# The weights of the last four experts taken by turns, parts of those with many tokens between parts of those with few

## The chip, the cores and the metric

The kernel runs on one core of one Trainium2 chip. The metric is the time of one execution on the device in microseconds (us). Three runs of the kernel before gave 1605.47, 1600.89 and 1598.26 us, with a median of 1600.89 us.

## What is computed

The reference is a small two-layer backbone for 256 latent tokens and 256 context tokens of width 1024. Each layer has a mixer (attention, pooling, retention) and a channel mixer. The channel mixer of the second layer is a mixture of eight experts, and it is the part that matters here:

```python
def moe_ffn(t, router, wg, wu, wd):
    tf = t.reshape(-1, shape[-1])
    logits = (tf @ router).astype(jnp.float32)
    top_v, top_i = lax.top_k(logits, TOP_K)
    top_w = jax.nn.softmax(top_v, axis=-1)
    gates = jnp.sum(jax.nn.one_hot(top_i, N_EXPERTS, dtype=jnp.float32) * top_w[..., None], axis=1)
    y = jnp.zeros_like(tf)
    for e in range(N_EXPERTS):
        y = y + gates[:, e:e + 1] * swiglu(tf, wg[e], wu[e], wd[e])
    return y.reshape(shape)
```

Every token goes to two of the eight experts. An expert is `(silu(t @ wg) * (t @ wu)) @ wd` with 1024 x 2816 weights in float32. After the experts come the residual and a layer norm, and the output.

## The kernel before, in words

All weights stream from HBM once. An expert is cut into FC = 11 **units**. Unit u has a gate and up part of 128 x 4096 floats (2 MiB, tile `rgu`) and a down part of 128 x 2048 floats (1 MiB, tile `raw`), so 3 MiB = 3.146 MB. There are two buffers of each, taken by the parity of u. `load_gu(u)` and `load_d(u)` issue the loads on the SP queue; the load for unit u + 2 is issued when unit u has given its buffer up, and SP takes the loads strictly in the order in which they are written.

The kernel counts the tokens of each expert on the chip and sorts the experts into eight **places** (`CNTI`, `POSM`, `GH`). A branch (`arms`, at the end of `build`) picks one of seven programs by these counts. Places 0 to 3 are done first; places 1, 2 and 3 are done together by `group(1, [2, 3], m, ...)`, which gives place 1 up to 256 tokens (two tiles of 128) and the two small ones m = 32 or 64 tokens, and which itself takes the weights of its three experts by turns. Places 4 to 7 follow. In the two programs in question places 4 and 7 have at most 64 tokens ("few") and 5 and 6 have up to 128 ("many").

The two kinds of unit load the engines in different ways:

- A **many** unit (M below) first splits its weights into two rounded parts: ACT copies (`ghi`, `dhi`), DVE subtracts (`glo`, `dlo`), in pieces of 128 x 1024 (`split_g`, `split_d`). PE then does three products for each tile (`mm3`): 24 matmuls of 512 columns for gate and up (`gate_up`), two transposes (`flips`), 12 matmuls of 512 columns for down (`down_to`). The buffers come free with the split, before PE has used the parts.
- A **few** unit (F below) is not split. PE multiplies the raw weights as they lie in the buffer (class `Few`: 32 matmuls of 64 x 256, one transpose, 8 of 64 x 512), so that the buffers come free only when PE has read them.

The order is written out by hand in `places(todo, side)`: for each place, for each c in range(FC), one unit: the splits, the first half of gate and up, the transposes of the unit behind, up to a few steps of side work (`aside`), the second half, the down product of the unit behind. Side work is a list of generators: `scatter` of a finished expert to its tokens, `gather` of the next expert's tokens into `XE[x]`, one-hot columns (`one_hot`), and at the end `closing` for the layer norm. With `few_ends = [(4, True), (5, False), (6, False), (7, True)]` the four last experts run one after the other: 11 F, 22 M, 11 F. For an F unit `places` does act, two steps of side work, turn and down within the same unit.

```python
                if few:
                    load_gu(u + 2)
                    if u < NU - 1:
                        act(u)
                        aside(2 if c < 9 else 8)
                        turn(u)
                        aside(1)
```

The tokens of place 4 and 7 come from a stash that `gather` filled before (`from_stash`).

## Time and profile before

| what | value |
|---|---|
| median of three runs | 1600.89 us |
| the profiled execution | 1599.23 us |
| its span, first to last instruction | 1597.4 us |
| mean granted clock of TensorE | 0.983 |
| PE busy | 1478.6 us (93%) |
| DVE busy | 743.9 us (47%) |
| ACT busy | 614.9 us (38%) |
| HBM read | 395.53 MB, 248 GB/s over the span |

The profiled execution lies 1.83 us above its span and 1.66 us below the median of the three runs. The shares are means over stages that differ: DMA stands at 40 to 50% in the first half of the span and near 90 to 100% from 860 us on, where the experts run. What the change is worth has to be read from the stretch of places 4 to 7, from 1177 us to the end. A busy PE is not a PE at its peak, because matmuls are pipelined and their ends are modelled, so periods between like instructions say more than busy time.

### The profile page before, as it was taken

What the parts mean: (1) busy time and instruction counts of PE and PEld (TensorE: products, weight loads), DVE (VectorE), ACT (ScalarE), POOL (GpSimd) and SP (SyncE); (2) the same over time, 40 slices, a digit from 0 to 9 for tenths busy, and PEclk for the clock granted to TensorE, in tenths of its full rate; (3) what the DMA queues carried; (4) which work ended last, traced back from release to release, by engine and by line L of the source; (5) the groups of instructions that cost most, each with busy time, mean ns of one, the idle gap of its engine ahead of it and who ended that gap; (6) DMA issues with size and microseconds to landing.
All of it is one profiled execution on the core that took longest, in us unless ns stands there. A gap on an engine that the chain in (4) does not pass through costs nothing. (4 is left out here: it accounts for less than half of the span.)

```text
span 1597.4 us, 25278 instructions
## 1 busy us (share of the span) xinstructions
PE 1478.6 (93%) x10388; PEld 1085.5 (68%) x10388; DVE 743.9 (47%) x1435; ACT 614.9 (38%) x1122; POOL 93.8 (6%) x105
## 2 busy tenths in 40 slices
PE   6989998999999999978988799999998889999986
PEld 4646777677777788775675577777765468877643
DVE  4564456332222353576555534344233078888412
ACT  3465444522222343255552223323220066767301
POOL 2310002000000240010000100000000000000120
PEclk9999999999999999999998899999999999999998
DMA  9445333554445332151368799999999998988894
GB/s 381 176 142 202 106 106 106 200 208 171 158 170 191 114 132 99 41 180 58 154 271 366 306 378 377 353 375 371 364 368 342 378 378 308 352 337 321 342 400 192
DMA packets 45699, 398.36 MB, mean 249 GB/s; under 512 B 5601, under 2 KB 5857, under 8 KB 8961
## 3 DMA queue, kind: packets, MB, share of 16 engines
q1 hardware_dynamic: 44640, 391.98, 64.5%
q0 software_dynamic: 640, 4.26, 0.7%
q8 instruction: 85, 1.39, 0.3%
q10 hardware_dynamic: 288, 0.36, 0.1%
q14 instruction: 46, 0.37, 0.1%
HBM read 395.53 MB, written 1.05 MB: 248 GB/s over the span
## 5 line engine op out<-in xcount | busy, mean ns | idle before, releaser
L281 PE MATMUL b<-HH,wh 128*128 128x512 f32 (+1 forms) x752 | 267.6, 356 | 7.8 <-ACT wh L281 6.4
L281 PE MATMUL b<-HH,wl 128*128 128x512 f32 (+1 forms) x752 | 258.7, 344 | 0.7 <-DVE wl L281 0.6
L281 PE MATMUL b<-HL,wh 128*128 128x512 f32 (+1 forms) x752 | 258.2, 343 | 1.1 <-DVE HL L281 1.1
L281 DVE TENSOR_TENSOR wl<-raw,wh 128x512 fp32r<-128x512 f32 x228 | 150.6, 702 | 124.6 <-ACT wh L281 124.4
L281 PE MATMUL bk<-ghi,HL 128*128 128x512 f32 x528 | 182.4, 408 | 8.4 <-ACT ghi L281 8.4
L281 PEld LDWEIGHTS b<-HH,wh 128*128 128x128 f32 x752 | 143.1, 190 | 64.7 <-issue 26.4
L281 ACT ACTIVATE wh<-raw 128x512 fp32r<-128x512 f32 x228 | 132.4, 622 | 117.7 <-DMA raw<-in_fgu_dram 56.9
L281 DVE TENSOR_TENSOR glo<-rgu,ghi 128x1024 fp32r<-128x1024 f32 x132 | 154.8, 1219 | 16.0 <-ACT ghi L281 15.9
L281 PEld LDWEIGHTS b<-HH,wl 128*128 128x128 f32 x752 | 143.2, 190 | 19.0 <-DVE wl L281 2.2
L281 PEld LDWEIGHTS b<-HL,wh 128*128 128x128 f32 x752 | 143.3, 191 | 17.2 <-DVE HL L281 1.9
L281 ACT ACTIVATE hx<-bk 128x256 f32<-128x256 f32 (+3 forms) x89 | 28.3, 318 | 304.6 <-PE bk L281 304.6
L281 ACT ACTIVATE ghi<-rgu 128x1024 fp32r<-128x1024 f32 x132 | 131.2, 1051 | 18.7 <-DMA rgu<-in_moe_dram 12.9
L281 DVE TENSOR_TENSOR hx<-hx,bk 128x256 f32<-128x256 f32 (+2 forms) x88 | 29.6, 336 | 232.2 <-ACT hx L281 232.2
L281 PEld LDWEIGHTS bk<-ghi,HL 128*128 128x128 f32 x528 | 101.7, 193 | 37.2 <-ACT ghi L281 9.5
L281 PE MATMUL bk<-dhi,SP 128*128 128x512 f32 x352 | 120.1, 402 | 0.0
L281 PE MATMUL b<-h,wh 128*128 128x512 f32 (+1 forms) x384 | 112.0, 376 | 0.0
L281 PE MATMUL bk<-glo,HL 128*128 128x512 f32 x264 | 105.5, 400 | 0.8 <-DVE glo L281 0.8
L281 DVE TENSOR_TENSOR H<-H,b 128x512 f32<-128x512 f32 x22 | 15.1, 688 | 168.4 <-PE b L281 158.3
L281 DVE TENSOR_TENSOR dlo<-raw,dhi 128x1024 fp32r<-128x1024 f32 (+1 forms) x55 | 78.8, 1434 | 15.8 <-ACT dhi L281 15.8
L281 PE MATMUL bk<-rgu,hx 128*32 128x128 f32 (+1 forms) x1376 | 77.1, 305 | 4.6 <-DVE hx L281 2.9
L281 PEld LDWEIGHTS b<-h,wh 128*128 128x128 f32 x384 | 69.9, 188 | 16.3 <-issue 2.5
L281 PEld LDWEIGHTS bk<-dhi,SP 128*128 128x128 f32 x352 | 66.1, 188 | 17.3 <-issue 1.6
(335 smaller groups left out, 2169.8 us busy)
## 6 DMA issues: line engine op xcount, KB each, us to landing
rgu<-in_moe_dram SPq DMA_DIRECT2D x81, 2048.0 KB, 9.7
raw<-in_moe_dram SPq DMA_DIRECT2D x80, 1024.0 KB, 7.4
raw<-in_wmod_dram SPq DMA_DIRECT2D x40, 1024.0 KB, 4.9
raw<-in_fgu_dram SPq DMA_DIRECT2D x22, 1024.0 KB, 6.0
p<-in_moe_dram SPq DMA_DIRECT2D x16, 1024.0 KB, 14.8
raw<-in_wout_dram SPq DMA_DIRECT2D x12, 1024.0 KB, 5.0
raw<-in_fd_dram SPq DMA_DIRECT2D x11, 1024.0 KB, 4.9
raw<-in_wib_dram SPq DMA_DIRECT2D x9, 1024.0 KB, 4.9
```

Of the source, the lines that this page charges most:

```text
L281: r = f(*args, **kw)
```

## The change

The two programs with `few_ends` no longer call `places`. A new function `by_turns` runs places 4 to 7. It first makes a list of the 44 units: 37 turns in which 22 M units (place 5, then 6) stand with 15 F units (place 4, then the first four of 7) spread evenly between them, then the last seven F units of place 7 alone:

```
M5.0 M5.1 F4.0 M5.2 F4.1 M5.3 M5.4 F4.2 M5.5 F4.3 M5.6 M5.7 F4.4 M5.8 F4.5 M5.9 M5.10 F4.6 M6.0
F4.7 M6.1 M6.2 F4.8 M6.3 F4.9 M6.4 M6.5 F4.10 M6.6 F7.0 M6.7 M6.8 F7.1 M6.9 F7.2 M6.10 F7.3
F7.4 F7.5 F7.6 F7.7 F7.8 F7.9 F7.10
```

Of the 37 turns 15 end with an F: eight pairs M F and seven triples M M F. The loop body is the one order for both kinds, with act, turn and down of a unit always one unit behind, also for F. If the unit after an F is an M, the first half of that M's split is issued during the F (`early`). The tokens of a few expert are gathered on the spot (`tokens_few`, 32 matmuls of 64 columns) and not from a stash. The accumulators of 4 and 7 move to banks 3 and 2; 5 and 6 share banks 0 and 1. `group` now hands over with place 5 as its next (128 slots for one expert where two copies of 64 slots stood).

```diff
-    def split_d(u, parts=1, eng=None):
+    def split_d(u, parts=1, eng=None, w=None):
...
+        def outer(u):
+            s, c = stream[u]
+            if light(u):
+                few_of(u).down(RD[u % 2], c)
+                load_d(u + 2)
+            else:
+                down_to(B[s], part[u] % 2, hts.pop(u), c)
+            if c == FC - 1 and s != 7:
+                side.append(scatter(s))
+                next(side[-1])
+                if s == 5:
+                    side.append(places_few(7))
...
+        side += [places_few(4), places_many(6)]
+        behind = None
+        early = set()
+        for u in range(u0, NU):
+            s, c = stream[u]
+            last = u == NU - 1
+            if light(u):
+                if c == 0:
+                    tokens_few(s)
+            elif u not in early:
+                run(split_g(u, 0, 2))
+            if behind:
+                act(behind)
+            inner(u, range(0, 4))
+            if not light(u):
+                run(split_g(u, 1, 2))
+                load_gu(u + 2)
+                rows = split_d(u, 2, w=part[u] % 2)
+                next(rows)
+            if behind:
+                turn(behind)
+            if light(u) and not last and not light(u + 1):
+                early.add(u + 1)
+                run(split_g(u + 1, 0, 2))
...
+            aside(4 if u == u0 else 3 if s == 7 and c > 3 else 2)
+            inner(u, range(4, 6))
+            if behind:
+                outer(behind)
+            inner(u, range(6, 8))
+            if light(u):
+                load_gu(u + 2)
+            else:
+                run(rows)
+            behind = u
...
-    def group(s, few, m, then):
+    def group(s, few, m, then, nxt=None, x=None):
...
-                  1: lambda: places(few_ends, group(1, [2, 3], 32, True)),
-                  2: lambda: places(few_ends, group(1, [2, 3], 64, True)),
+                  1: lambda: by_turns(lambda: group(1, [2, 3], 32, False, 5, 0)),
+                  2: lambda: by_turns(lambda: group(1, [2, 3], 64, False, 5, 0)),
```

How the order moves, first on PE at the start of an F unit. Before, in place 4 (`rgu` and `raw` are the raw weights, `os` the one-hot columns of a scatter, `CA` the identity of a transpose):

```order
L281 MATMUL bk_6521<-rgu_5029,hx 64x256 x8
L281 MATMUL bk_6521<-rgu_5029,sil 64x256 x8
L281 MATMUL bk_6522<-os_6505,SP 128x256 x4
L281 MATMUL bk_6520<-os_6506,SP 128x256 x4
L281 MATMUL bk_6521<-CA,hx 128x128
L281 MATMUL bk_6522<-os_6506,SP 128x256 x4
L281 MATMUL bk_6515<-raw_79,hx 64x512 x4
```

Now, in an F of the turns, with the last products of the M ahead of it and the down product of that M (`dhi`, `dlo`) within it (three of its 12 matmuls are shown, the others read alike):

```order
L281 MATMUL bk_6519<-ghi_8973,HL 128x512
L281 MATMUL bk_6521<-rgu_5029,hx 64x256 x8
L281 MATMUL bk_6519<-CA,hx 128x128 x2
L281 MATMUL bk_6520<-og,HH 128x128 x8
L281 MATMUL bk_6521<-rgu_5029,sil 64x256 x4
L281 MATMUL bk_6515<-dhi_8977,SP 128x512
L281 MATMUL bk_6515<-dlo_8979,SP 128x512
L281 MATMUL bk_6516<-dhi_8977,SP 128x512
L281 MATMUL bk_6521<-rgu_5029,sil 64x256 x4
L281 MATMUL bk_6519<-ghi_8971,HL 128x512
```

The gate and up product of an F stood in one piece; now the transposes, a step of side work and the 12 down matmuls of the M ahead stand between its pieces.

Second, the SP queue, with what each load waits for (the row between two loads, which only forms an address, is left out). Before, in the M stage:

```order
L281 DMA rgu1_6304<-in_moe_dram 128x4096 [waits DMAHW5_49,DVE_49]
L281 DMA raw0_78<-in_moe_dram 128x2048 [waits DMAHW6_49,DVE_49]
L281 DMA rgu0_5029<-in_moe_dram 128x4096 [waits DMAHW7_49,DVE_49]
L281 DMA raw1_79<-in_moe_dram 128x2048 [waits DMAHW0_49,DVE_49]
L281 DMA rgu1_6304<-in_moe_dram 128x4096 [waits DMAHW1_49,DVE_49]
```

Now, over pairs M F:

```order
L281 DMA rgu1_6304<-in_moe_dram 128x4096 [waits DMAHW1_49,PE_49]
L281 DMA rgu0_5029<-in_moe_dram 128x4096 [waits DMAHW3_49,DVE_49]
L281 DMA raw0_78<-in_moe_dram 128x2048 [waits DMAHW2_49,PE_49]
L281 DMA raw1_79<-in_moe_dram 128x2048 [waits DMAHW4_49,DVE_49]
L281 DMA rgu1_6304<-in_moe_dram 128x4096 [waits DMAHW5_49,PE_49]
L281 DMA rgu0_5029<-in_moe_dram 128x4096 [waits DMAHW6_49,DVE_49]
```

Every second load waits for PE instead of DVE, and the down part of an F stands behind the gate and up part of the M after it.

Third, DVE at an F between two M, now (`glo` and `dlo` are splits, `hx` the activation, `SP` the split of the turned activation, `XT` the rows that a scatter adds to):

```order
L281 TENSOR_TENSOR hx<-hx,bk_6519 128x256 [waits Activation_49]
L281 TENSOR_TENSOR SP<-bk_6519,SP 128x256 [waits Activation_49]
L281 TENSOR_TENSOR glo_8976<-rgu_6304,ghi_8973 128x1024 [waits DMAHW4_49,Activation_49]
L281 TENSOR_TENSOR glo_8976<-rgu_6304,ghi_8973 128x1024 [waits Activation_49]
L281 TENSOR_TENSOR XT<-XT,bk_6520 128x2x256 [waits PE_49]
L281 TENSOR_TENSOR XT<-XT,bk_6522 128x2x256 [waits PE_49]
L281 TENSOR_TENSOR hx<-hx,bk_6521 128x128 [waits Activation_49]
```

The first half of the next M's split, which waits for that M's load, now stands ahead of the additions of a scatter and of the F's own activation.

## Rows read from the trace of the kernel before

**Rows 1.** Stages: the group, F of 4, M, F of 7, tail.
```profile
core 0: us, PE busy (x) PEld busy (x) DVE busy (x) ACT busy (x) POOL busy (x), PEclk, DMA share, GB/s
924.00:1177.00 253.00, 252.31 (x2520) 189.27 (x2516) 96.93 (x146) 79.78 (x120) 0.00 (x0) 1.00 0.93 366
1177.00:1281.00 104.00, 91.35 (x702) 54.07 (x690) 21.32 (x60) 10.63 (x27) 0.00 (x0) 0.98 0.95 369
1281.00:1481.00 200.00, 190.60 (x873) 153.21 (x870) 166.81 (x187) 139.28 (x176) 0.00 (x0) 0.98 0.89 339
1481.00:1561.00 80.00, 71.51 (x473) 42.38 (x473) 20.12 (x37) 14.57 (x27) 13.06 (x16) 1.00 0.95 373
1561.00:1597.00 36.00, 23.12 (x165) 13.38 (x161) 9.22 (x25) 5.90 (x15) 0.00 (x0) 0.88 0.42 170
```

**Rows 2.** SP queue in time: issue of `rgu` for units 44, 55, 77, 87.
```profile
1177.47 0.33 SPq L281 DMA_DIRECT2D rgu<-in_moe_dram  x1
...
1281.36 0.33 SPq L281 DMA_DIRECT2D rgu<-in_moe_dram  x1
...
1480.84 0.33 SPq L281 DMA_DIRECT2D rgu<-in_moe_dram  x1
...
1561.40 2.06 SPq L281 DMA_DIRECT2D rgu<-in_moe_dram  x2
```

**Rows 3.** Waits of the SP queue, 1290 to 1490 us (total, times, longest).
```profile
SPq L281 <- DVE glo L281: 98.4, 22, 5.9
SPq L281 <- DVE dlo L281: 81.9, 21, 5.6
```

**Rows 4.** The page: few experts' products in the group (32 slots).
```profile
L281 PE MATMUL bk<-rgu,hx 128*32 128x128 f32 (+1 forms) x1376 | 77.1, 305 | 4.6 <-DVE hx L281 2.9
```

**Rows 5.** SP queue in time: `rgu` loads in the group, three units apart.
```profile
939.83 0.82 SPq L281 DMA_DIRECT2D rgu<-in_moe_dram  x1
...
964.43 0.96 SPq L281 DMA_DIRECT2D rgu<-in_moe_dram  x1
...
989.09 0.33 SPq L281 DMA_DIRECT2D rgu<-in_moe_dram  x1
```

**Rows 6.** PE in time, one M unit (start us, us, engine).
```profile
1369.64 0.38 PE L281 MATMUL bk<-CA,hx 128*128 128x128 f32 x2
...
1372.63 0.40 PE L281 MATMUL bk<-dhi,SP 128*128 128x512 f32 x1
...
1375.44 0.39 PE L281 MATMUL bk<-ghi,HL 128*128 128x512 f32 x1
...
1378.20 0.38 PE L281 MATMUL bk<-CA,hx 128*128 128x128 f32 x2
```

**Rows 7.** PE in time, F units that run free.
```profile
1260.75 0.33 PE L281 MATMUL bk<-CA,hx 128*128 128x128 f32 x1 [0.70 <-DVE hx L281]
1261.46 1.94 PE L281 MATMUL bk<-raw,hx 128*64 128x512 f32 x8 [0.38 <-DVE hx L281]
1263.23 1.90 PE L281 MATMUL bk<-rgu,hx 128*64 128x256 f32 x16
1264.95 1.90 PE L281 MATMUL bk<-rgu,sil 128*64 128x256 f32 x16
1267.55 0.33 PE L281 MATMUL bk<-CA,hx 128*128 128x128 f32 x1 [0.70 <-DVE hx L281]
```

**Rows 8.** PE in time: two scatter steps in one row.
```profile
1200.79 1.21 PE L281 MATMUL bk<-os,SP 128*128 128x256 f32 x8
```

**Rows 9.** DVE in time: two pieces of a split.
```profile
1372.56 2.35 DVE L281 TENSOR_TENSOR glo<-rgu,ghi 128x1024 fp32r<-128x1024 f32 x2
```

**Rows 10.** SP queue in time: `rgu` loads five units apart in place 7.
```profile
1517.80 0.33 SPq L281 DMA_DIRECT2D rgu<-in_moe_dram  x1
...
1554.02 0.33 SPq L281 DMA_DIRECT2D rgu<-in_moe_dram  x1
```

**Rows 11.** Stage view, 20 us within place 7.
```profile
1540.00:1560.00 20.00, 17.52 (x129) 8.83 (x131) 1.45 (x5) 3.31 (x7) 0.00 (x0) 1.00 1.00 425
```

More of the change, by code (lines that the diff above doesn't have):

```diff
@@ L1524, in split_g @@
                 load_gu(u + 2)
-    def split_d(u, parts=1, eng=None):
+    def split_d(u, parts=1, eng=None, w=None):
         if u < NU:
+            w = u % 2 if w is None else w
             n = 2048 // parts
@@ L1530, in split_d @@
                 c = slice(n * j, n * j + n)
-                split(RD[u % 2][:, c], DHI[u % 2][:, c], DLO[u % 2][:, c], eng)
+                split(RD[u % 2][:, c], DHI[w][:, c], DLO[w][:, c], eng)
                 yield ("rest",)
@@ L2246, in group @@
             units += [(1 + i // FC, i % FC) for i in range(len(few) * c, len(few) * c + len(few))]
-        stream.update({u0 + i: (([s] + few)[j], c) for i, (j, c) in enumerate(units)})
-        end = u0 + len(units)
+        own = {u0 + i: (([s] + few)[j], c) for i, (j, c) in enumerate(units)}
+        stream.update(own)
         part.update({u0 + n * c: u0 + c for c in range(FC)})
-        nxt = s + 1 + len(few)
-        x = nxt % 2
+        if nxt is None:
+            nxt = s + 1 + len(few)
+            x = nxt % 2
         side = []
@@ L2388, in group @@
                 run(split_d(u + n))
-        stream.clear()
-        part.clear()
+        for u in own:
+            del stream[u]
+            part.pop(u, None)
         if len(few) == 1:
@@ L2540, in next_first @@
         run(split_d(FC))
-    few_ends = [(s, s in (4, 7)) for s in (4, 5, 6, 7)]
     def two_groups():
```

89 lines of the change are left out of this document (added).

## The prediction, made before the changed kernel was run

> **What bounds the kernel now.** I read the stage view first [rows 1], because the change touches only places 4 to 7, then the SP queue for when each load is issued [rows 2], then what SP waits for [rows 3], then PE's rows for the price of one unit [rows 6, 7]. The program that runs is the one with 32 slots, as the 128*32 form of the group's few products shows [rows 4], and it is one of the two that call the new function, so that the change does take effect.
>
> From the load of unit 44 to that of unit 87, the last, 383.9 us pass (1177.47 to 1561.40), 43 steps of 8.93 us [rows 2]. They fall apart into three pieces: 11 F units of place 4 in 103.9 us (9.44 each), 22 M units in 199.5 us (9.07 each), ten F units of place 7 in 80.6 us (8.06 each). Behind the last load 36.0 us are left to the end of the span.
>
> In the M piece PE is the bound: it is busy 190.6 of 200 us while DMA stands at 0.89 and moves 339 GB/s [rows 1]. There SP waits 98.4 us for the gate and up splits and 81.9 us for the down splits, at nearly every load [rows 3]. The splits in turn wait for buffers that PE still reads. One M unit takes PE 8.56 us, from one pair of transposes to the next [rows 6]; 22 of these are 188.3 us of the 199.5.
>
> In the F pieces it is the other way round. PE needs less: the down product 1.77 us, the two halves of gate and up 1.72 and 1.90, the transpose 0.33, so 5.7 us [rows 7], and idles between for activation and copy on other engines. DMA stands at 0.95 [rows 1], and at best moves 425 GB/s [rows 11]. So one stage leaves DMA waiting for PE, the other PE waiting for DMA, and the change lays them over each other.
>
> **The change part by part.** *Prices in the turns.* For DMA I take the group, which already mixes both kinds of work with the same buffers: six units in 49.26 us, 8.21 each or 383 GB/s [rows 5]. For PE: M 8.56, F 5.7, and the side work, about 45 steps in all (scatters of six results, gathers, one-hot columns) at 0.6 us by the scatter's row [rows 8], 27 us in all or 0.7 for each of the 37 turns.
>
> *A pair M F* then asks PE for 8.56 + 5.7 + 1.4 = 15.7 us and DMA for 16.4. *A triple M M F* asks PE for 22.8 + 2.1 = 24.9 and DMA for 24.6. The two are nearly equal, so neither hides fully behind the other, and I add 0.3 us to a triple for the handover. Eight pairs at 16.4 and seven triples at 25.2 are 307.6 us.
>
> *Does the buffer of an F come free in time?* It is the new wait: SP's next load for that buffer now stands behind PE. From the start of the F, PE does 1.8 us of gate and up, two transposes, some 1.2 us of side work, 0.9 of gate and up, the 12 down matmuls of the M ahead (2.81, from 1372.63 to 1375.44 [rows 6]) and 0.9 again, 7.9 us with the transposes. Behind the F's gate and up part three loads lie ahead in the queue: the next M's gate and up, the F's down part and that M's down part, 2 + 1 + 1 MiB of 3 MiB a unit, so 4/3 x 8.21 = 10.9 us. That leaves 3 us, enough for an issue but not for a stall. Queued behind the waiting load on SP are the next M's gate and up part and both down parts.
>
> *The early split.* ACT and DVE now stand at the next M's load while the F runs. Behind them wait a scatter's additions and the F's own activation, which is needed only a unit later. A gather that follows its one-hot columns in the same step would make PE wait for the split as well. There are three such places. Each costs from 0 to 4.6 us: the M's load lands when PE is half through the F, and four pieces of split and the columns must pass, two of them 2.35 us [rows 9].
>
> *Gathering on the spot* for places 4 and 7: twice 32 matmuls of 64 columns and two copies. By columns (2048, as in the eight matmuls of rows 8) 1.2 us each, by matmuls (0.15 each) 4.8. For both kinds of one-off together I take 8 us out of 2.4 to 23.4, since PE has some slack in a pair.
>
> *The last seven F alone.* Free of scatters, place 7 shows five steps in 36.22 us, 7.24 each [rows 10]. The new loop keeps one unit behind, so that PE no longer waits for activation and copy inside a unit (0.70 and 0.38 us [rows 7]); six steps of 7.24 are 43.4 us.
>
> *Edges.* The hand-over from the group gathers 128 slots for one expert instead of twice 64, the same matmuls. The first M must be split before PE can start, but its load was issued as early as before; 0, with -2 to +3 us. The tail has the same instructions, 36.0 us; the additions on POOL (13.06 us [rows 1]) have two units of 7 us before they are read. The bookkeeping in `group` costs nothing, it is done when the program is built.
>
> **Sum.** 307.6 + 8 + 43.4 = 359.0 us in place of 383.9: 24.9 us less. The profiled execution took 1599.23 us, so 1574.3; the median of the runs is 1.66 above it, and I predict **1576 us**. From here on all times are against that median.
>
> A rule speaks against this. The Trainium skill, page "DMA: Bandwidth & Descriptors", section Specifications, puts the share of HBM for one core at about 358 GB/s. By it a unit costs 8.79 us at best, the 43 steps 378 us, and with the one-offs nothing is won. The trace does not agree with it as a limit: rows 11 show 425 GB/s, rows 5 383.
>
> **Rivals.** *A: memory is already the limit.* The 43 steps carry 43 x 3.146 MB in 383.9 us, 352 GB/s. If that is what memory gives while the vector engines work, then no order helps: 0 gained, 1601 us. For it: place 4 shows 369 GB/s at a DMA share of 0.95 [rows 1], so the engines were busy and yet slow. Against it: rows 5, 10 and 11, and SP's waits for splits in the M stage [rows 3]. The rule above would put the time here as well.
>
> *B: slower, by the early split.* If in each F the steps of side work made PE wait for the split of the next M, the F's buffer would come free 4.6 us later than the 3 us in hand allow, and DMA would stand still. Fifteen times 4.6 is 69 us; against the 24.9 gained, 44 us more: 1645 us. It turns to a loss from six of the 15 F units on. For it: the order on DVE, where a scatter's additions stand behind the split. Against it: side work uses two banks in turn and two steps at a time, so PE mostly writes without waiting for the addition just queued.
>
> *C: more than forecast.* If loads run at rows 11's rate whenever issued, PE is the only bound: 22 x 8.56 + 15 x 5.7 + 27 = 300.8, with 43.4 for the rest 344.2, 39.7 less: 1561 us. Against it: PE and the loads would have to fit without a gap.
>
> **How the numbers follow.** The forecast has 0.73, C 0.09, A 0.11, B 0.07. A measurement of this kernel can tell about 0.5% (8 us) from no change. Forecast and C are faster: 0.82. A is the same: 0.11. B is slower: 0.07. The forecast's own range is 1568 to 1594: 1576 with the one-offs at 2.4 or 23.4 us and the edges at -2 or +3. C at 1561 and a margin of 3 us set the low end, 1558. The high end is 1596, which leaves A and B out, 0.18.
>
> **What would show it.** Right: the load of unit 87 some 25 us earlier after that of unit 44; in the turns a mean of about 8.5 us a unit, DMA above 0.93 and near 370 GB/s, PE above 0.93; 7.0 to 7.4 us for a unit at the end; a tail of 36 us. Wrong: DMA at 0.95 or more with 355 GB/s and PE idle (A); SP's gate and up loads waiting for PE with DMA under 0.9, and PE waiting for DVE in the F units (B).

## The result, and the profile after

The changed kernel takes 1678.61 us (median of four runs, 1677.53 to 1680.32), the kernel before 1603.18 us in its four runs. The ratio is 1.0469, with a 95% interval from 1.0442 to 1.0496: **slower by 4.7%**, where 1576 us had been forecast. The profiled execution took 1677.53 us, its span 1675.7.

First a slip in the rows ahead of the prediction. The load at 1281.36 in [rows 2] is that of unit 56; unit 55 was issued at 1273.97. So place 4 took 96.5 us (8.77 a unit) and the M stage 206.9 us (9.40 a unit), and PE's 188.3 us stand against 206.9. The sum of 383.9 us stands.

The stages of the kernel after by the stage view, for [rows 1]: the group, the hand-over, the turns, six F alone, and the last stretch.

```profile
924.00:1177.00 253.00, 252.31 (x2513) 189.12 (x2513) 97.09 (x147) 79.76 (x120) 0.00 (x0) 1.00 0.93 368
1180.00:1215.00 35.00, 30.32 (x223) 22.27 (x215) 18.54 (x27) 15.49 (x23) 0.00 (x0) 0.95 0.83 318
1215.00:1600.00 385.00, 336.29 (x1621) 219.56 (x1621) 189.05 (x250) 143.12 (x192) 1.76 (x3) 0.92 0.72 290
1600.00:1640.00 40.00, 32.79 (x214) 16.41 (x212) 3.00 (x9) 3.87 (x9) 11.31 (x14) 0.87 0.85 332
1640.00:1676.00 36.00, 22.02 (x151) 12.23 (x147) 9.23 (x25) 5.91 (x15) 0.00 (x0) 0.86 0.40 149
```

The group is what it was. In the turns PE is busy for only 336 of 385 us, DMA has fallen to a share of 0.72 and 290 GB/s, and the granted clock to 0.92. Neither side is the bound; each waits for the other. From the load of unit 44 (1180.43) to that of unit 87 (1640.56) 460.1 us pass, against 383.9 before and 359.0 forecast.

What SP waits for from 1200 to 1600 us (total, times, longest), for [rows 3]:

```profile
SPq L281 <- PE bk L281: 229.5, 29, 20.7
SPq L281 <- DVE glo L281: 85.4, 22, 6.6
SPq L281 <- DVE dlo L281: 29.5, 7, 5.9
```

The loads now wait mostly for PE, 229.5 us in all. In the M stage before they waited for splits alone [rows 3], but in the F stages they waited for PE too: in the kernel before from 1177 to 1281 and from 1481 to 1561 us, and, for comparison, in e12 (below), whose turns come close to the forecast, from 1190 to 1540 us:

```profile
SPq L281 <- PE bk L281: 92.8, 24, 7.0
SPq L281 <- PE bk L281: 57.6, 16, 6.6
SPq L281 <- PE bk L281: 198.1, 40, 10.5
```

So a long wait of SP for PE is not the loss in itself. What counts is whether DMA runs dry meanwhile, and whether what is issued then comes in time. How it fails is seen in one pair and the triple behind it, which carry no side work. The SP queue in time:

```profile
1345.04 0.33 SPq L281 DMA_DIRECT2D rgu<-in_moe_dram  x1
1351.05 0.33 SPq L281 DMA_DIRECT2D raw<-in_moe_dram  x1
1362.15 3.98 SPq L281 DMA_DIRECT2D rgu<-in_moe_dram  x2
1369.14 0.91 SPq L281 DMA_DIRECT2D raw<-in_moe_dram  x2
1378.02 3.98 SPq L281 DMA_DIRECT2D rgu<-in_moe_dram  x2
1385.02 0.91 SPq L281 DMA_DIRECT2D raw<-in_moe_dram  x2
1391.93 0.33 SPq L281 DMA_DIRECT2D rgu<-in_moe_dram  x1
1396.99 0.33 SPq L281 DMA_DIRECT2D raw<-in_moe_dram  x1
1408.72 0.33 SPq L281 DMA_DIRECT2D rgu<-in_moe_dram  x1
```

and the stage view around the holes (us, then PE, PEld, DVE, ACT, POOL, granted clock, DMA share, GB/s):

```profile
1356.00:1361.00 5.00, 5.00 (x30) 3.06 (x26) 2.79 (x3) 2.28 (x3) 0.00 (x0) 1.00 0.02 10
1370.60:1401.30 30.70, 26.43 (x118) 17.17 (x117) 15.88 (x18) 13.41 (x17) 0.00 (x0) 0.94 0.98 407
1401.30:1409.00 7.70, 7.70 (x49) 4.75 (x49) 4.48 (x6) 4.31 (x8) 0.00 (x0) 1.00 0.07 29
```

The F start at 1354.8, 1370.64 and 1401.35 us. From 1351 to 1362 and from 1397 to 1409 SP stands at one gate and up load whose buffer the F is to be multiplied from, and issues nothing. What was issued before has landed by then, and DMA does next to nothing (0.02, 0.07). In the triple that begins with the F at 1370.64 it is the other way: the loads run at 407 GB/s and still come late. The second M's gate and up part takes the F's buffer and goes out at 1378.02, when the F's last product is done, together with another load; its down part takes the F's down buffer, which is multiplied only one unit later, and goes out at 1385.02. The PE rows of this triple:

```profile
1370.64 1.95 PE L281 MATMUL bk<-rgu,hx 128*64 128x256 f32 x16
1391.57 0.62 PE L281 MATMUL bk<-ghi,HL 128*128 128x512 f32 x2
1394.56 0.50 PE L281 MATMUL bk<-dhi,SP 128*128 128x512 f32 x1 [1.92 <-ACT SP L281]
1395.88 0.84 PE L281 MATMUL bk<-dhi,SP 128*128 128x512 f32 x2 [0.59 <-DVE SP L281]
1396.95 1.06 PE L281 MATMUL bk<-dhi,SP 128*128 128x512 f32 x2
1401.35 1.95 PE L281 MATMUL bk<-rgu,hx 128*64 128x256 f32 x16
```

and ACT's:

```profile
1385.85 2.00 ACT L281 ACTIVATE ghi<-rgu 128x1024 fp32r<-128x1024 f32 x2 [3.54 <-DMA rgu<-in_moe_dram]
1393.18 1.06 ACT L281 ACTIVATE dhi<-raw 128x1024 fp32r<-128x1024 f32 x1 [3.16 <-DMA raw<-in_moe_dram]
1394.14 0.37 ACT L281 ACTIVATE SP<-bk 128x256 fp32r<-128x256 f32 x1
```

The gate and up part is there 7.8 us after its issue, the down part 8.2 us after its own. ACT stands at the late down part with the turned activation (`SP`) queued behind it, and PE stands for ACT. After this wait two products of 512 columns take 1.06 us (1396.95) where two took 0.62 before it (1391.57). From F to F the triple takes 30.7 us; forecast were 25.2.

An F with side work in it gives its gate and up buffer up much later still. In nine of the 15 F of the turns the next load goes out 7.4 us after the F's start. In the second, third and fourth F of place 4 it is 14.8, 15.7 and 15.0 us, because PE stands within the F for an addition, one-hot columns or a copy that wait on DVE behind two pieces of the early split:

```profile
1254.58 1.29 PE L281 MATMUL bk<-os,og 32*128 32x256 f32 x4 [3.81 <-DVE XT L281]
1297.22 1.95 PE L281 MATMUL bk<-og,HH 128*128 128x128 f32 x8 [4.01 <-DVE og L281]
1323.77 0.59 PE L281 MATMUL bk<-GH,og 128*128 128x2 f32 x2 [4.23 <-DVE os L281]
```

Some of the F alone at the end wait for their loads, and this one starts at half rate (1.90 us for sixteen products in [rows 7]):

```profile
1604.64 3.58 PE L281 MATMUL bk<-rgu,hx 128*64 128x256 f32 x16 [2.27 <-DMA rgu<-in_moe_dram]
```

### The profile page after: what moved, and what is told of

Same layout as the page of the kernel before. It is cut to its first block, busy times and chain, and to the rows that moved or that the text cites. A ratio compares the mean times of both kernels' runs of the same rounds, so it can differ in the third digit from the quotient of the medians.

```text
span 1675.7 us, 25208 instructions
## 1 busy us (share of the span) xinstructions
PE 1527.3 (91%) x10388; PEld 1094.9 (65%) x10388; DVE 746.0 (45%) x1437; ACT 613.6 (37%) x1116; POOL 93.9 (6%) x105
## 4 chain that ended last, share of the span: by engine, by line
PE 35%; DMA 6%; DVE 6%; ACT 2%; issue 1%; SPq 0%; DVEq 0%; ACTq 0%
PE bk L281 35%; DMA raw<-in_moe_dram 4%; DVE glo L281 2%; DMA rgu<-in_moe_dram 2%; DVE dlo L281 1%; ACT ghi L281 1%; DVE XT L281 1%; ACT dhi L281 0%; DVE rgu L281 0%; DVE hx L281 0%; ACT hx L281 0%; DVE SP L281 0%; DVE os L281 0%; DVE kept L281 0%; ACT SP L281 0%
## 5 line engine op out<-in xcount | busy, mean ns | idle before, releaser
L281 PE MATMUL bk<-ghi,HL 128*128 128x512 f32 x528 | 188.0, 415 | 10.6 <-ACT ghi L281 10.6
L281 PEld LDWEIGHTS b<-HL,wh 128*128 128x128 f32 x752 | 144.3, 192 | 17.2 <-DVE HL L281 1.9
L281 PE MATMUL bk<-dhi,SP 128*128 128x512 f32 x352 | 130.2, 432 | 13.3 <-ACT SP L281 11.3
L281 PEld LDWEIGHTS bk<-dhi,SP 128*128 128x128 f32 x352 | 70.7, 202 | 42.1 <-ACT SP L281 13.5
L281 PE MATMUL bk<-rgu,hx 128*32 128x128 f32 (+1 forms) x1376 | 84.4, 317 | 8.4 <-DMA rgu<-in_moe_dram 6.8
L281 DVE TENSOR_TENSOR H<-H,b 128x512 f32<-128x512 f32 x22 | 15.1, 688 | 169.6 <-PE b L281 158.6
L281 PEld LDWEIGHTS b<-h,wh 128*128 128x128 f32 x384 | 69.8, 188 | 16.4 <-issue 2.5
```

What stands on the lines that cost most here:

```text
L281: r = f(*args, **kw)
```

## The experiments

All times below from one run stand beside one run of the kernel before on the same chip (1597.74 to 1607.67 us), so the periods in the traces say more than differences of a few us: up to the load of unit 44 all these kernels do the same, and yet it goes out anywhere from 1176.4 to 1183.9 us. "43 steps" is the time from the load of unit 44 to that of unit 87. Kernels with e1's edit ask for that last load earlier within its unit (some 42 us are left behind it in place of 35), so the 43 steps show them some 7 us too good. "To the end" is the time from the load of unit 44 to the end of the span; it is free of both: 495.3 us in the change, 419.9 in the kernel before, 395.0 by the forecast (359.0 and 36.0).

### First round: one suspect at a time

**e1, the F's product in one piece, its next load right behind.**

```diff
-            inner(u, range(0, 4))
+            inner(u, range(0, KT if light(u) else 4))
...
+            else:
+                load_gu(u + 2)
```

> The changed kernel took 1678.6 us; in it the 37 turns take 402 us and the last six steps 58 us (issue of the gate and up load of unit 44 to that of unit 87). Theory H (held buffer): a unit with few tokens gives its gate and up buffer up only at its very end, behind the down product of the unit ahead (2.8 us) and the side work, so that loads are issued late and in a burst and PE starves. Here its gate and up product stands in one piece and its load right behind it. H expects the triples M M F to fall by about 3 us each and the last units from 9.7 to about 7.4 us: some 35 us less, about 1643 us. Theory Q (vector queue): PE starves because the early split of the next unit stands on DVE and ACT ahead of the side work. Q expects a gain only at the end, some 12 us: about 1666 us.

Measured: 1646.82 us, 32 less; to the end 468.4, 26.8 less. The total is near theory H, but not by the way H gave: clean triples (those without side work) stay at 30 to 30.4 us. The F's down buffer still comes free a unit late, and the second M's down part with it. In such a triple of e1 ACT and PE stand as in the change:

```profile
1376.19 1.06 ACT L281 ACTIVATE dhi<-raw 128x1024 fp32r<-128x1024 f32 x1 [4.42 <-DMA raw<-in_moe_dram]
1377.58 0.50 PE L281 MATMUL bk<-dhi,SP 128*128 128x512 f32 x1 [3.21 <-ACT SP L281]
```

So the late gate and up load is about a quarter of the miss, and half of what the last F lost (from the load of unit 81 to the end 93.1 us in the change, 85.9 here, 79.4 forecast), but not what the clean triples lose.

**e2, no side work in an F ahead of an M, three steps instead of two elsewhere.**

```diff
-            aside(4 if u == u0 else 3 if s == 7 and c > 3 else 2)
+            aside(4 if u == u0 else 3 if s == 7 and c > 3 else 0 if light(u) and not last and not light(u + 1) else 3)
```

> Side work is taken out of the units with few tokens that come before one with many, where the early split stands ahead of it on DVE, and is done in the others (3 steps instead of 2). Q expects the waits of PE for og, XT, os and HL on DVE (25 us in the turns) to go, and part of the lost clock with them: about 1645 us. H expects the buffer of a few unit to come free some 1.2 us earlier where a step stood ahead of it, in all at most 10 us: about 1668 us.

Measured: 1658.31 us, 20 less, between the two; to the end 15.1 less. In the three F that gave their buffer up after 14.8 to 15.7 us it is 7.4 now.

**e3, fifteen pairs and then seven M in a row.**

```diff
-            units.append((many_ if -(-2 * FC * (i + 1) // turns) > -(-2 * FC * i // turns) else few_).pop(0))
+            units.append((many_ if i % 2 == 0 or i >= 2 * (turns - 2 * FC) else few_).pop(0))
```

> The 37 turns stand as 15 pairs M F and then 7 M, in place of 8 pairs and 7 triples. In the changed kernel a pair without side work takes 15.9 to 17.1 us, a triple 29.7 to 31.0. H says that a triple loses since the load of its second M is issued only when the F ahead ends, one unit before it is needed: 7 triples less 5.3 us each, about 1641 us. Q, for which the number of F units counts, expects 1678 within 8 us.

Measured: 1657.75 us, 21 less, between the two (17.6 to the end): the triples are dear, but not the whole miss.

**e4, no early split.**

```diff
-            if light(u) and not last and not light(u + 1):
+            if False:
```

> The early split is left out: the first half of a many unit's split is issued in that unit itself, as for the other ones. Q expects the waits of PE for DVE in the few units to go: 20 to 40 us less, about 1650 us. H expects each of the 15 many units behind a few unit to start with a wait for its first pieces of split (2.3 us) and its own buffer to come free as much later: up to 35 us more, about 1710 us.

Measured: 1667.43 us, 11 less (13.5 to the end). The early split costs something; the price that was set for going without it didn't come.

### Second round: do they add up?

**e5, e1 to e3 together.**

> The three edits of the first runs together: gate and up of a few unit in one piece with its load behind it, no side work behind an early split, 15 pairs and then 7 many units. Alone they took 31.8, 20.3 and 20.9 us off 1678.6. If they remove different waits they add up to 1606 us. If two of them (one piece, pairs) remove the same one, the late load of the second many unit, some 1625 us.

Measured: 1631.36 us, 47 less where the three alone gave 73. Of these 26 us of overlap 11 lie ahead of the load of unit 44, where the edits do nothing. To the end it is 47.0 less, where the three alone gave 59.5: an overlap of some 12 us, so that they remove the same waits in part.

**e6, an F ahead of an M ends within itself**: its activation, transpose and down product come at once, and its down part is asked for ahead of the next M's loads.

```diff
+            if light(u) and not last and not light(u + 1):
+                inner(u, range(0, 4))
+                if behind:
+                    turn(behind)
+                inner(u, range(4, 8))
+                load_gu(u + 2)
+                act(u)
+                if behind:
+                    outer(behind)
+                turn(u)
+                aside(1)
+                early.add(u + 1)
+                run(split_g(u + 1, 0, 2))
+                outer(u)
+                behind = None
+                continue
```

> A few unit that comes before a many unit ends within itself: its activation, turn and down product, the load of its next down part, and one step of side work are all written ahead of the early split of the next unit; the order of units is that of the change. H and Q together expect the gain of the first run (to 1647 us) and, since down parts are loaded earlier and nothing but the next unit stands behind the early split, most of PE's remaining waits there (ACT SP 14, DVE og 12, XT 5, os 5 us): about 1615 us. If it stays at 1640 or more, neither the late down parts nor the order on the vector engines is what is left.

The F alone at the end keep e1's edit.

Measured: 1614.92 us, 64 less than the change, by the order alone. The 43 steps take 393.2 us; to the end it is 435.0, 60.2 less. Clean pairs take 15.2 us, clean triples 24.8 and 25.0. One clean triple of e6 in the stage view, beside the one above that took 30.7 us:

```profile
1338.30:1363.30 25.00, 23.94 (x120) 16.35 (x119) 15.80 (x18) 13.30 (x17) 0.00 (x0) 1.00 1.00 393
```

DMA is at 1.00 throughout. The load for the F's buffer goes out 4.2 us after the F's start (in the change 7.4), the one for its down buffer 9.7 after (in the change 14.4):

```profile
1342.53 0.33 SPq L281 DMA_DIRECT2D rgu<-in_moe_dram  x1
1347.96 0.33 SPq L281 DMA_DIRECT2D raw<-in_moe_dram  x1
```

What is left above the forecast are the turns with side work: pairs of 17.2 to 17.5 us, the pair with the tokens of place 7 23.6, triples of 29.1 to 34.1.

**e7, e6 with the pairs of e3.** Part of one scatter works on other data here; the work is the same.

> The same with 15 pairs and then 7 many units. If the triples still lose by a late load, another 15 to 20 us less than the run before, about 1598 us; if the loads are now early enough, the same as the run before within 5 us.

Measured: 1615.34 us, the same as e6. Once the F ends within itself, triples are no worse than pairs.

**e8, the changed kernel with 24 of the 32 products left out of the two gathers of tokens.**

```diff
-            for k in range(KT):
+            for k in (0, 7):
```

> The changed kernel with 24 of the 32 matmuls left out that gather the tokens of a few expert on the spot, for places 4 and 7 (so their tokens are not gathered and these two experts work on stale data). In the trace they took 3.65 and 6.51 us. Taken away, some 8 us less if they are on the path, up to 15 if the lower clock behind them goes too: 1664 to 1671 us. Not on the path: 1678 us.

Measured: 1662.64 us, 16 less; to the end 12.5 less. This gather stands on the path. Its rows in the change, at place 4 with the F behind it and at place 7, and last the F behind the shortened gather of place 4 in e8:

```profile
1221.51 3.65 PE L281 MATMUL bk<-HL,HH 128*128 128x64 f32 x32
1225.63 3.63 PE L281 MATMUL bk<-rgu,hx 128*64 128x256 f32 x16 [0.47 <-ACT hx L281]
1515.12 6.51 PE L281 MATMUL bk<-HL,HH 128*128 128x64 f32 x32 [1.57 <-DVE HL L281]
1220.61 1.95 PE L281 MATMUL bk<-rgu,hx 128*64 128x256 f32 x16 [0.47 <-ACT hx L281]
```

### Third round: the price of side work

**e9, the changed kernel without side work in the turns.**

```diff
-        side = begin()
+        begin()
+        side = []
...
-        side += [places_few(4), places_many(6)]
```

> The changed kernel with the side work of the turns left out: the steps that the group hands over, the one-hot columns and gathers of places 4 to 7, and the scatters of places 4, 5 and 6. Only the on-the-spot gathers of tokens, the last scatter and the closing stay, so the output is not the reference's. The order of units, splits, products and loads is as changed. Theory S (side work is not hidden: each step stands where the F's buffer is waited for, or ahead of it on DVE, and so costs more than its time on PE): pairs of the kind that run clean in the changed kernel, 16.0 us, everywhere, and triples of 30.2, so eight times 16.0 and seven times 30.2 = 339 us with the two gathers of tokens some 350 in place of 402 for the turns; the time about 50 us less, 1625 to 1632. Theory H (side work costs its time on PE, 45 times 0.6 = 27 us, as the forecast had it): 1650 to 1654. If it were hidden: 1675 or more.

Measured: 1626.11 us, 52 less, and the 43 steps take 412.2 (to the end 447.2, 48.0 less). Theory S. Pairs are 15.8 to 16.1 us everywhere (one, with the tokens of place 7, 20.0), triples 29.5 to 32.6.

**e10, e6 with the tokens gathered ahead as side work.**

```diff
-            og, b = ogs[s], BK[7]
+            og, b = ogs[s], B[s][0]
...
+                if k % 2:
+                    yield
```

> The kernel whose F ahead of an M ends within itself (1614.9 us, e6), with the tokens of places 4 and 7 gathered ahead, step by step as side work, into the idle accumulator bank of that expert; only the two copies stay at the first F. Theory O (the gather on the spot costs because PE waits for its one-hot columns and its copies in one place, with no load going out): 12 to 16 us less than e6 for the two, 1599 to 1603. Theory P (it is PE time, wherever it stands): 1610 to 1615.

Measured: 1620.75 us; to the end 441.4, where e6 has 435.0. Not theory O, and above the range of theory P: the pair with the tokens of place 7 falls from 23.6 to 16.6 us, but the turns that now hold its steps grow by as much or more (29.4 to 34.0, 15.2 to 17.4).

**e11, three F of place 4 ahead of the turns.** A bank that the group's last scatter still reads is written early here; the work is the same.

> As e10 for place 7, but three F of place 4 stand ahead of the turns, so that 34 turns are left (22 M, 12 F) and the side work that the group hands over falls where F stand alone and PE has time to spare. If side work is what keeps e6 above its forecast, and not the mixing: 1595 to 1605. If an F alone costs what the last seven do (7.2 us with the loads as bound) and side work costs the same anywhere: 1608 to 1616. The kernel before on the same chip is what it stands against.

Measured: 1612.38 us, in the second of the two ranges: side work costs about the same there. The 43 steps, 392.0 us, are those of e6.

**e12, e6 without side work**: the edits of e6 and e9.

> The kernel whose F ahead of an M ends within itself (e6, 1614.9 us), with the same side work left out as in e9, so that the output is not the reference's. Theory S (what keeps e6 above its forecast is side work alone, and the two causes add up): every pair 15.2 and every triple 25.0 as in e6's clean turns, 297 us with the tokens some 305 in place of 352 for the turns, and the time 1565 to 1575. Theory M (pairs and triples are dearer for another reason while the group's rest drains, such as DMA or the banks that 5 and 6 share): the first turns stay at 17 and 31 to 34 us, and the time is 1590 or more.

Measured: 1586.32 us, 11 above the upper end of theory S and below theory M. The pairs are as expected, 15.2 and 15.3 us, the triples 24.8 to 26.9, the one pair with tokens 19.3; the 37 turns, by their loads, take 318.7 us where some 305 had been expected (and 315.6 forecast). The 43 steps take **359.6 us; the forecast was 359.0**. That flatters it: to the end it is 401.5 us against 395.0, since 41.9 us follow the last load in place of 36.0. Besides, the load of unit 44 goes out at 1183.11 us, 5.6 later than before. The stage view over the turns, first of e9, from its first F to the last of the turns:

```profile
1218.20:1536.60 318.40, 283.91 (x1366) 179.84 (x1366) 163.53 (x192) 134.29 (x175) 0.00 (x0) 0.97 0.81 327
```

and the same stretch of e12, with the same instructions:

```profile
1225.00:1504.90 279.90, 267.90 (x1368) 178.67 (x1368) 161.63 (x192) 134.01 (x175) 0.00 (x0) 0.99 0.94 372
```

With the F ended within itself DMA stands at 0.94 and PE at 268 of 280 us: both near full, as forecast. And 12 us of idle PE are too little room for 27 us of side work (the forecast's estimate).

Why a step costs more than its products is seen in e6's rows. PE by line, the sided triple from 1240.7 to 1274.7 us (busy, mean ns of one | idle before and what ended it):

```profile
L281 PE MATMUL bk<-ghi,HL 128*128 128x512 f32 x33 | 13.2, 463 | 0.0
L281 PE MATMUL bk<-os,og 32*128 32x256 f32 x16 | 2.4, 333 | 1.8 <-DVE XT L281 1.7
L281 PE MATMUL bk<-IDR,og 128*128 128x128 f32 x2 | 0.4, 302 | 1.9 <-DVE XT L281 1.9
L281 PE MATMUL bk<-GH,og 128*128 128x2 f32 x2 | 0.4, 260 | 0.5 <-DVE os L281 0.5
```

and the clean one from 1338.3 to 1363.3:

```profile
L281 PE MATMUL bk<-ghi,HL 128*128 128x512 f32 x33 | 11.0, 397 | 0.0
```

DVE in time, in the sided triple:

```profile
1249.09 4.62 DVE L281 TENSOR_TENSOR glo<-rgu,ghi 128x1024 fp32r<-128x1024 f32 x4
1253.63 1.22 DVE L281 TENSOR_TENSOR dlo<-raw,dhi 128x1024 fp32r<-128x1024 f32 x1
1254.77 0.74 DVE L281 TENSOR_TENSOR XT<-XT,bk 128x256 f32<-128x256 f32 x2
```

and the stage view of the 6 us behind the first wait:

```profile
1256.00:1262.00 6.00, 6.00 (x21) 4.70 (x22) 4.58 (x6) 2.36 (x5) 0.00 (x0) 0.72 0.94 332
```

Of the 9 us between the two triples PE is busy for 5.8 (29.71 against 23.94 us) and idle for 3.2 (4.2 us of waits against 1.0). The busy part is 3.2 us of side products and some 3.6 us by which the same weight products take longer (the `ghi` alone 2.2); the groups overlap a little, so that they add up to more than 5.8. PE waits because a scatter's addition to `XT`, which gives the bank back, stands behind five pieces of split on DVE (1249.09 to 1254.77). After the wait the granted clock is 0.72 over 6 us.

**e13, the steps of an M issued one by one, later in the unit.**

```diff
-            aside(4 if u == u0 else 3 if s == 7 and c > 3 else 2)
+            aside(4 if u == u0 else 3 if s == 7 and c > 3 else 2 if light(u) else 0)
...
+            if heavy_side:
+                aside(1)
```

The last two lines stand twice, ahead of the down product of the unit behind and after the last quarter (`heavy_side`: an M that isn't the first unit).

> e6 with the same side work, but the two steps of an M are issued one by one, between the last quarters of its gate and up product and behind them, in place of both in a row right behind its splits. Theory D (a step is dear because its addition stands behind the splits on DVE, so that PE waits 1.7 to 1.9 us for a bank at the next step and then runs at the lower clock): the waits of PE for XT and og go, sided triples fall from 29 to 34 us to 27 to 29, and the time to 1598 to 1606. Theory W (side work costs its matmuls and DVE time wherever it stands): 1612 to 1617.

Measured: 1611.34 us, just below theory W's range; the 43 steps 388.0 us, 5.2 less than e6. PE's waits for `XT` and `og` are gone from the turns, as D said, but the gain is well below what D gave: in their place stand 8.4 us of waits for splits (`glo`, 3.7 in e6), and sided triples still take 28 to 32 us.

### Last round: what is left of the order by turns

**e14 and e15, e13 with the tokens of place 7 gathered ahead.** In both the gather for place 4 is left out: it was tied to the first unit, and the first F is the third unit. e15's expectation, written before this was seen, blames a bank.

```diff
+                    if u == u0:
+                        run(tokens_few(s))
+                    tokens_copy(s)
```

> e13 (1611.3 us, and 13.6 above the kernel before on the same chip) with the tokens of place 7 gathered ahead as side work into the idle accumulator bank, as in e10. The pair that holds this gather falls from 22.2 to about 17 us, so 4 to 6 us less than e13. Theory L (loads and PE are both near their limit in the turns, and side work, hidden by the slack of PE in the F stages of the kernel before, has to be paid for there): it stays 5 to 12 us above the kernel before. If the order by turns still held a gain that only stalls take away: below the kernel before.

> As e14, but the tokens of place 4 go to the bank that the change uses for them, since the group's last scatter still reads the other one, which e14 overwrites. The same work in the same order: 1600 to 1606 us, ratio to the kernel before 0.996 to 1.004 (theory L: the gain of the order and the price of the side work cancel). A ratio below 0.995 would speak for a gain that is left in the order by turns.

Measured: e14 1602.98 us, ratio 0.9998 [0.9978, 1.0017]; e15 1602.17 us, 0.9995 [0.9980, 1.0010]. Level with the kernel before, with some work missing.

**e16, e15 with three F of place 4 first** (here the first F is the first unit, and its tokens are gathered).

> e15 with three F of place 4 ahead of the turns, as in e11, so that part of the side work stands where PE has slack. If that is what the side work lacks in the turns: 4 to 10 us less than e15, 0.993 to 0.998 of the kernel before. If an F alone with side work costs as much as it saves: the same as e15 within 3 us.

Measured: 1614.34 us, ratio 1.0068 [1.0044, 1.0091]. Part of what it has above e15 is the gather, but e17 below, with the same work, is lower still. Taking F out of the turns for side work gains nothing.

**e17, e15 with the gather for place 4 back.** The edit against e15:

```diff
-                    if u == u0:
+                    if s == 4:
```

> e15 does not gather the tokens of place 4 at all (32 matmuls, two copies, in the first F); here they are gathered as in the changed kernel, so that no work is left out. By the 16 us for most of two such gathers in the changed kernel (e8), and the 5 for one in a mended pair (e13's 22.2 against e14's 16.9), 5 to 8 us more than e15: 1607 to 1611, ratio to the kernel before 1.003 to 1.006. Theory L (the side work that PE's slack hid before keeps the order by turns above the kernel before): above 1.002 with its whole interval. If the order still held a gain: at or below 1.000.

Measured: 1608.22 us beside 1603.48, ratio **1.0032 [1.0020, 1.0043]**. Theory L had asked for an interval above 1.002; its lower end lies right there. With all the work done and the stalls that the traces show mended as far as was tried, the order by turns is 0.3% above the kernel before. No version here that does all the work beats it.

## Why the prediction was wrong

The miss is 101.1 us in the 43 steps (460.1 against 359.0) and 100.3 to the end (495.3 against 395.0). Two edits account for 93.8 of these 100.3, whichever comes first:

| | 43 steps, us | to the end, us | less to the end |
|---|---|---|---|
| the change | 460.1 | 495.3 | |
| e6, F ends within itself | 393.2 | 435.0 | 60.2 |
| e12, and no side work | 359.6 | 401.5 | 33.6 |
| e9, no side work alone | 412.2 | 447.2 | 48.0 |
| e12, and F ends within itself | 359.6 | 401.5 | 45.8 |
| forecast | 359.0 | 395.0 | |

From e9 to e12 no side work is left that could stand behind the early split, so its 45.8 us are the price of the late buffers alone. That e12 meets the 43 steps to 0.6 us is in part luck: 6.4 us stay to the end.

**The step that failed first is "Does the buffer of an F come free in time?"** Its time on PE, 7.9 us with 1.2 us of side work, holds only where there is none: 7.4 us in nine of the 15 F (1370.64 to the issue at 1378.02), but 8.3 to 15.7 us in the six others, where side work, waits for DVE or the lower clock come in; e2, without side work there, has 7.4 in four of these six. In a clean pair its queue was right too: at 1365.80 and 1369.14 the three loads that it counts go out, they run until the F ends, and the pair costs no more than was forecast. In a triple it fails at two points, side work or not. First, it asked only whether DMA would run dry, not when the next load is wanted. In a pair the unit that takes an F's buffers is the next F, which needs no split; in a triple it is the second M, which must have its weights and split them within the 8.56 us of the first M; its gate and up part was there 7.8 us after the F's end, and the split still to come. Second, it followed the gate and up buffer alone and named the down parts only as "queued behind". The F's down product had been moved one unit behind, so that its down buffer came free 14.4 us after the F's start, and the second M's down part arrived 8.2 us later, when PE stood for it. The late triple then delays the next F, whose loads ahead are only two (issued at 1391.93 and 1396.99, the F at 1401.35), so that SP stands and DMA has its hole of 7.7 us. e1 mends the gate and up buffer, e6 both.

**"I add 0.3 us to a triple for the handover"** is a consequence of the same step, not a price of its own: triples took 29.7 to 30.7 us where clean, and 24.8 to 25.0 in e6, where 25.2 had been forecast. The clean pairs were better than forecast, 15.8 to 16.1, in e6 15.2, against 16.4, and for another reason than given: not the loads are their bound but PE, which is busy for 14.82 of 15.20 us in each clean pair of e6, with DMA anywhere from 0.75 to 1.00. But the forecast was to hold with side work, and sided pairs took 22.4 and 25.3, sided triples 33.6 to 42.9.

**Side work was taken as hidden.** With 0.7 us a turn, PE's sum (15.7 in a pair) stayed just under that of DMA (16.4), and in a triple it was level with it (24.9 and 24.6), and so the 27 us were counted at next to nothing. A sum of busy times on PE has no room for what happens between the engines. In e6 side work costs 33.6 us, in the change, where it also holds up the F's buffers, 48.0: its products and the waits and slower products around them. In the kernel before, the F stages have PE busy for only 91.35 of 104 us [rows 1] and had room for it. That these stages hid it then was not run as an experiment of its own; that the turns don't is what e9 and e12 show.

**"The early split"** was a range of 0 to 4.6 us at three places. Three such stalls are there, of 3.81, 4.01 and 4.23 us, though only the one at 1297.22 is a gather behind its one-hot columns. As waits they lie within the range; what it left out is that the F's buffer comes free some 7 us later each time. e4, which leaves the early split out, gains 13.5 us to the end, e2, which takes side work out of these F, 15.1.

**"Gathering on the spot"**: 1.2 to 4.8 us each, taken together with the stalls at 8 of at most 23.4. The products alone took 3.65 and 6.51 us, PE also waits, and the F behind them starts at half rate (3.63 us for sixteen products). For place 4 that makes some 5.8 us, for place 7 more; leaving out three quarters of both gathers' products gives back 12.5 us to the end (e8). So each is dearer than the upper bound of 4.8.

**"The last seven F alone"**: 9.7 us each by the loads in place of 7.24, and 8.9 from F to F. The next load was issued only after all of an F's product; with e1's edit it is 7.8 from F to F, in e6 7.5.

**The edges were right** in the change: 35.1 us from the last load to the end, 36.0 forecast; the load of unit 44 went out 3.0 us later, at the bound of the range given and within its scatter from run to run.

**Rivals.** A falls: the turns of e12 have 372 GB/s with splits running, against A's 352. The Trainium skill, page "DMA: Bandwidth & Descriptors", section Specifications, with its 358 GB/s for a core, would have allowed none of this; the trace disagrees, with 407 GB/s over 30.7 us. B had the right sign and the right sort of thing: F buffers that come free late, with DMA under 0.9. Its price, 69 us for the F in all, is near the 60.2 that e6 takes away, but by luck, since its cause was mostly another: steps of side work behind the early split held up three F out of 15 and cost some 13.5 to 15.1 us (e4, e2); most of the rest are the two loads written behind the whole product and behind the next unit. Its time of 1645 us was 33 too low. It had been given 0.07 on the ground that PE "mostly writes without waiting", which speaks of the split alone.

A page of the Trainium skill names just this kind of change: "Perfetto Trace Analysis", section Optimization Strategy, says that where the engine that limits a kernel changes from one stretch to the next, interleaving the stretches may help. The runs agree as far as e12, which leaves work out and takes 401.5 us to the end against 419.9 before, and not beyond: with the side work back the order only comes near the kernel before (e17, 1.0032).

What stays open is the split of the 33.6 us into products, waits and clock over all turns; it was read for one triple. Open too are the 6.4 us by which e12 stays above the forecast, and how much of the 45.8 us belongs to each of the two buffers: e1 mends one of them, but with side work in the turns. A third buffer for the F's weights was not tried.

## What to carry to other kernels

Before mixing units whose buffers come free at different times, write down for each load when it is issued, what it waits for, and what stands behind it on its queue: one load that waits for a late reader stops every load behind it, and the unit that takes the buffer may be the next but one, with one unit's time to land and be split. Count the time until a buffer comes free with the side work in it, and with what that side work waits for. A few us of such waiting per unit outweigh what two well-matched busy sums promise. Where the mixed stages come out nearly full on both engines, ask where the side work will go that the old stages had room for. Ending the slow reader's unit at once (e6) gave back 60 of the 75 us that the change had lost, with the same instructions in another order.

## What the runs showed of the hardware that was not expected

- A wait of PE can cost more than its length. After 1.7 us of waiting the granted clock was 0.72 over the next 6 us (e6, 1256 to 1262), that is, part of them at the lower of its two levels, 1.2 GHz; after 2.27 us sixteen products took 3.58 us instead of 1.90, at a clock of 0.53 (the change, 1604.6 to 1608.2). Over the turns the clock was 0.92 in the change, 0.99 in e12. The Trainium skill, page "TensorE: Matmul & The Clock Gate", section "HAM oscillation — how this bites in real kernels", describes a loop in which each wait for a load puts PE back to its lower clock. The second of these waits is one for a load and agrees with it; the first is one for DVE, and not every wait here had that price: behind 2.19 us that end at 1431.01 in the change the clock was 1.00 over the next 8 us.

- The clock also fell behind products, with hardly a wait. In the change 32 products of 64 columns keep PE busy from 1221.51 at a clock of 1.00, 0.47 us of waiting follow, and then the clock is 0.53 (1225.6 to 1229.2). In e8, which leaves 24 of the 32 out, it is 1.00 over the same sixteen products of the F (1220.6 to 1222.5).
- Mixed turns with their stalls mended get as much from memory as the F stage before: 372 GB/s over the turns of e12, 369 before at place 4 [rows 1].
